# Taking the root of the query and key norms in two parts in a hybrid attention layer

## The chip, the cores and the metric

One Trainium2 chip, one core. The metric is the device time of one execution in microseconds; the times of the kernel before are 1372.91, 1371.18 and 1371.32 us, their median 1371.32 us. Engines are named as the profile names them: PE is TensorE (PEld its weight loads), DVE is VectorE, ACT is ScalarE, POOL is GpSimd, SP is SyncE, from whose queue nearly all DMAs are issued.

## The reference, cut to what matters

One decoder layer on 2048 tokens of width 1024: a pre-norm, one input projection, three attention branches side by side (latent attention with 8 heads, differential attention with 4 heads of two maps, cross-attention into 256 memory tokens), a gate, and one output projection. In the latent and in the differential branch every query and every key of every head is divided by the root of its mean square before (rotation and) the scores. These are the norms of this change:

```
def rms_norm(x, g, eps=RMS_EPS):
    xf = x.astype(jnp.float32)
    y = xf * lax.rsqrt(jnp.mean(xf * xf, axis=-1, keepdims=True) + eps)
    return (y * g.astype(jnp.float32)).astype(x.dtype)
# latent branch: heads of 64 plain and 32 rotated columns
    k = jnp.concatenate([k_nope, k_rope], axis=-1)
    q = rms_norm(q, qn_g)
    k = rms_norm(k, kn_g)
    q = jnp.concatenate([q[..., :MLA_NOPE], rope(q[..., MLA_NOPE:], pos)], axis=-1)
    k = jnp.concatenate([k[..., :MLA_NOPE], rope(k[..., MLA_NOPE:], pos)], axis=-1)
# differential branch: 8 maps of 32 columns
    q = rms_norm(dq.reshape(b, s, DIFF_HEADS * 2, DIFF_D), qn_g)
    k = rms_norm(dk.reshape(b, s, DIFF_HEADS * 2, DIFF_D), kn_g)
    q = rope(q, pos).reshape(b, s, DIFF_HEADS, 2, DIFF_D)
    k = rope(k, pos).reshape(b, s, DIFF_HEADS, 2, DIFF_D)
```

The inverse root doesn't depend on the rotation, so it can be multiplied on after it.

## The kernel before, in words

The work is cut into 28 steps: four blocks of 512 tokens for the memory branch (m), for two pairs of differential heads (d, 8 steps) and for four pairs of latent heads (a, 16 steps), in that order. Each step has a preparation (`prep_d`, `prep_a`) and then its attention maps. The maps run on PE (scores L572 or L917 to L919, values L516, L518, L536), ACT (the exponential p, L506) and DVE (its low half plo, L507). Beside them run the projections (L187 to L189), the gates, and late in the kernel the output projection (L958 to L960).

A preparation projects queries, keys and values, squares them (ACT), sums the squares (DVE) and takes the inverse root in `rstd_of` (L91 to L102) on POOL: one instruction adds the epsilon (L97) and one raises to the power -0.5 (L101). Then:

- `prep_d` (differential): the sums of 8 maps of queries and 8 of keys for 4 x 128 tokens lie in one tile of 32 columns, ss_d (L441). Keys are rotated first, then queries, on DVE (L354 to L358), each with a table that POOL makes (rt_d, L332 to L335); the table has one buffer, so that of the queries can be made only when the keys are rotated. One root for all 32 columns (r_d) stands between the two in the program. Then DVE multiplies the keys by it (L457), ACT and DVE split them into high and low halves (s_d, L465 and L466), SP transposes them by DMA (kT_d, L474), and the same follows for the queries (qB_d).
- `prep_a` (latent): the sums lie in ss_a, 8 columns of queries (L857) and 8 of keys (L854). POOL rotates the queries (L354 to L358), adds the part of the shared rotated key (L862), takes one root of 16 columns (r_a), and multiplies the rotated key by its 8 (L867, into kn_a). DVE multiplies the rest of the keys (L871) and then the queries (L873). Per head, ACT copies the high half of keys (ks_a, L878) and DVE takes the low half (L879), SP transposes (kT_a, L882), and so for queries (qs_a, L885 and L886, qB_a, L891).

After that the preparation estimates the largest score per query (`est_block`: PE L398, ACT L404 and L407, DVE L408 to L413), writes it into the queries, and transposes these again (L484, L900). Only then are the maps of the step free to start.

The order of the instructions on every engine is planned when the program is built, by priorities (a preparation goes ahead of what comes later in the list) and by planned times; on the chip every engine then works its own list strictly in that order, and waits where an operand isn't there. Preparations, maps and fills are woven into each other by due times (`Task`, L1110 onwards); a preparation is due 11 units (`LEAD`) ahead of its maps.

Of the kernel before, what the change touches and what calls it, by code (L numbers as in the profile page):

```python
# [11 lines left out]
F32 = mybir.dt.float32  # L12
# [4 lines left out]
ALU = mybir.AluOpType  # L17
AX = mybir.AxisListType

P = 128  # L20
# [12 lines left out]
def _bc(ap, axis, n):  # L33
    ap = ap.unsqueeze(axis)
    shape = list(ap.shape)
    shape[axis] = n
    return ap.broadcast_to(shape)
# [3 lines left out]
def hybrid_block(ctx: ExitStack, tc: tile.TileContext, x, mem, positions, norm_g, w_in, mla_q_norm_g,  # L41
# [3 lines left out]
    V, A, G, T, SP = nc.vector, nc.scalar, nc.gpsimd, nc.tensor, nc.sync  # L45
# [5 lines left out]
    sm = ctx.enter_context(tc.tile_pool(name="sm", bufs=2))  # L51
# [6 lines left out]
    def stack(shape, name):  # L58
        return wk.tile(shape, F16, tag="s2", name=name, bufs=6)
# [29 lines left out]
    gm = gain_cols(mem_norm_g, NK, "gm", WS, G)  # L89

    def rstd_of(ss, shape, name, tag="rstd", eps=EPS):  # L91
        r = sm.tile([P, 32 if tag == "rstd" else 8], F32, tag=tag, name=name)
        n = int(np.prod(shape))
        rv = r[:, 0:n]
        if len(shape) == 2:
            rv = rv.rearrange("p (a b) -> p a b", b=shape[1])
        G.tensor_scalar(rv, ss, eps, None, ALU.add)  # L97
        m = mhalf
        if len(shape) == 2:
            m = m.unsqueeze(2)  # L100
        G.tensor_tensor(rv, rv, m.broadcast_to([P] + list(shape)), ALU.pow)  # L101
        return rv  # L102
# [246 lines left out]
    def rope_in_place(q, tb, nh, eng, tmp):  # L349

        tmp = tmp.rearrange("p (t h d) -> p t h d", t=4, d=32)
        C = _bc(tb[:, 0], 2, nh)
        Sn = _bc(tb[:, 1], 2, nh)
        eng.tensor_tensor(tmp[..., 0:16], q[..., 16:32], Sn[..., 0:16], ALU.mult)  # L354
        eng.tensor_tensor(tmp[..., 16:32], q[..., 0:16], Sn[..., 16:32], ALU.mult)
        eng.tensor_tensor(q, q, C, ALU.mult)
        eng.tensor_tensor(q[..., 0:16], q[..., 0:16], tmp[..., 0:16], ALU.subtract)
        eng.tensor_tensor(q[..., 16:32], q[..., 16:32], tmp[..., 16:32], ALU.add)  # L358
# [18 lines left out]
    def new_qb(shape, name):  # L377
        return wk.tile(shape, F16, tag="qB", name=name, bufs=5)
# [45 lines left out]
    def prep_d(st, units):  # L424
        g, b, nm = st.g, st.b, st.name
# [14 lines left out]
        ss = sm.tile([P, 32], F32, tag="ss", name=f"ss_{nm}")  # L440
        V.reduce_sum(ss, sq.rearrange("p (a d) -> p a d", d=32), axis=AX.X)  # L441
        yield 1.0
        for w, gain in ((1, g_dk), (0, g_dq)):
            r4 = qk[:, :, 128 * w:128 * w + 128].rearrange("p t (m d) -> p t m d", d=32)
            rope_in_place(r4, rope_tabs(b, gain, f"{nm}{w}"), 4, V, sq[:, 512 * w:512 * w + 512])
            if w:
                r = rstd_of(ss, [32], f"r_{nm}").rearrange("p (t m) -> p t m", m=8)
            yield 2.0
        yield 1.0
        yield 1.0  # L450
# [3 lines left out]
        for w in (1, 0):  # L454
            r3 = qk[:, :, 128 * w:128 * w + 128]
            r4 = r3.rearrange("p t (m d) -> p t m d", d=32)
            V.tensor_tensor(r4, r4, _bc(r[:, :, 4 * w:4 * w + 4], 3, 32), ALU.mult)  # L457
            yield 1.0
            for i in range(2):
                dst = stack([P, 4, 2, 4, 32], f"s{w}{i}_{nm}")  # L460
                src = r4[:, :, 2 * i:2 * i + 2, :]
                G.memset(dst[:, :, :, 3, :], MS if w else 0.0)
                at_hi, at_lo = ((0, 2), 1) if w else ((0, 1), 2)
                for k in at_hi:
                    A.activation(dst[:, :, :, k, :], src, AF.Copy)  # L465
                V.tensor_tensor(dst[:, :, :, at_lo, :], src, dst[:, :, :, 0, :], ALU.subtract)  # L466
                if w:
                    out = kT[:, i].rearrange("p t m k -> p (t m) k")
                else:
                    qB = new_qb([P, 4, 2, P], f"qB{i}_{nm}")  # L470
                    st.qs.append(dst)
                    st.qB.append(qB)
                    out = qB.rearrange("p t m k -> p (t m) k")
                SP.dma_start_transpose(out, dst.rearrange("p t m r d -> p (t m r d)"))  # L474
                yield 1.0
# [348 lines left out]
    def prep_a(st):  # L824
        g, b, nm = st.g, st.b, st.name
# [24 lines left out]
        ss = sm.tile([P, 2, 8], F32, tag="ssa", name=f"ss_{nm}")  # L850
# [9 lines left out]
        rope_in_place(q[..., 64:96], tb, 2, G, sqt[:, 768:1024])  # L860
        s4 = ss[:, 1, :].rearrange("p (t h) -> p t h", h=2)
        G.tensor_tensor(s4, s4, _bc(ss_kr[b], 2, 2), ALU.add)  # L862
        r = rstd_of(ss.rearrange("p a b -> p (a b)"), [16], f"r_{nm}")
        rq = r[:, 0:8].rearrange("p (t h) -> p t h", h=2)
        rk = r[:, 8:16].rearrange("p (t h) -> p t h", h=2)
        yield 1.0
        G.tensor_tensor(kn[..., 64:96], _bc(krot[b], 2, 2), _bc(rk, 3, 32), ALU.mult)  # L867
        yield 1.0
        yield 1.0
        yield 1.0  # L870
# [227 lines left out]
    def a_prep(st):  # L1098
        if st.g == 0 and st.b == 0:
            yield from load_a_weights()  # L1100
        yield from prep_a(st)
# [102 lines left out]
    while True:  # L1204
# [26 lines left out]
        else:  # L1231
            mp, j, p0, h = heads.pop(0)
# [31 lines left out]
```

## Time and profile before

| | |
|---|---|
| median of the times | 1371.32 us |
| the profiled execution's own time | 1372.15 us |
| its span, first to last instruction | 1370.3 us |
| PE busy | 1293.0 us (94%) |
| DVE busy | 1123.1 us (82%) |
| ACT busy | 903.9 us (66%) |
| POOL busy | 333.9 us (24%) |
| mean granted TensorE clock | 0.989 |

Busy shares are means over stages with different limits. The memory steps and the loading of weights fill the first 150 us, the maps of the differential heads run until about 800 us with the preparations up to 640 us, and the preparations of the latent heads run from 640 to 1250 us. An engine's idle time costs something only where it makes PE, or the engine that PE waits for, stand.

### The profile page before, as it was taken

What the parts mean: (1) busy time and instruction counts of PE and PEld (TensorE: products, weight loads), DVE (VectorE), ACT (ScalarE), POOL (GpSimd) and SP (SyncE); (2) the same over time, 40 slices, a digit from 0 to 9 for tenths busy, and PEclk for the clock granted to TensorE, in tenths of its full rate; (3) what the DMA queues carried; (4) which work ended last, traced back from release to release, by engine and by line L of the source; (5) the groups of instructions that cost most, each with busy time, mean ns of one, the idle gap of its engine ahead of it and who ended that gap; (6) DMA issues with size and microseconds to landing.
All of it is one profiled execution on the core that took longest, in us unless ns stands there. A gap on an engine that the chain in (4) does not pass through costs nothing.

```text
span 1370.3 us, 35041 instructions
## 1 busy us (share of the span) xinstructions
PE 1293.0 (94%) x13616; PEld 829.5 (61%) x13616; DVE 1123.1 (82%) x2713; ACT 903.9 (66%) x2163; POOL 333.9 (24%) x477
## 2 busy tenths in 40 slices
PE   5988999999999999999998999999999998999998
PEld 2434556667667767667775656666655665655554
DVE  4657888879889867889899889999998998886745
ACT  6656544677878646786896667677766877665521
POOL 2322232403042133113202143223243323200000
PEclk9999999999999999999999999999999999999999
DMA  7998844223113322447446166347525643275452
GB/s 231 199 208 184 184 111 101 59 60 88 41 25 71 79 34 60 78 110 193 124 98 144 40 167 150 84 107 167 109 71 118 145 99 55 40 155 158 141 184 70
DMA packets 294262, 155.52 MB, mean 113 GB/s; under 512 B 239952, under 2 KB 272848, under 8 KB 294096
## 3 DMA queue, kind: packets, MB, share of 16 engines
q1 hardware_dynamic: 294064, 153.29, 47.7%
q8 instruction: 106, 1.74, 0.5%
q14 instruction: 60, 0.49, 0.1%
q0 software_dynamic: 32, 0.00, 0.0%
HBM read 61.75 MB, written 34.34 MB: 70 GB/s over the span
## 4 chain that ended last, share of the span: by engine, by line
PE 56%; DVE 13%; POOL 9%; ACT 8%; DMA 8%; issue 4%; SPq 1%; ACTq 0%; DVEq 0%; POOLq 0%
PE pp L189 6%; PE pp L187 6%; PE pp L188 6%; PE pe L398 5%; DVE plo L507 4%; PE pv L518 3%; PE pv L516 3%; PE pv L536 3%; PE st L572 3%; PE pp L958 3%; PE pp L959 3%; PE pp L960 3%; PE st L917 3%; PE st L918 2%; PE st L919 2%
## 5 line engine op out<-in xcount | busy, mean ns | idle before, releaser
L506 ACT ACTIVATE p<-st 128x512 f32<-128x512 f32 (+3 forms) x672 | 356.2, 551 | 167.2 <-PE st L919 65.8
L507 DVE TENSOR_TENSOR plo<-p 128x512 f16<-128x512 f32 (+3 forms) x672 | 404.6, 615 | 63.1 <-ACT p L506 59.2
L407 ACT ACTIVATE ec<-pe 128x512 bf16<-128x512 f32 (+3 forms) x384 | 197.2, 536 | 39.2 <-PE pe L400 17.1
L516 PEld LDWEIGHTS <-p 128*128 128x128 bf16 x2304 | 186.0, 99 | 51.5 <-DVE y_a L924 4.7
L518 PEld LDWEIGHTS <-p 128*128 128x128 bf16 x2304 | 173.1, 98 | 39.4 <-issue 4.1
L408 DVE TENSOR_TENSOR er<-er,ec 128x512 bf16<-128x512 bf16 (+3 forms) x384 | 141.5, 378 | 29.9 <-ACT ec L407 15.2
L404 ACT ACTIVATE er<-pe 128x512 bf16<-128x512 f32 x192 | 110.0, 606 | 47.2 <-DVE mx_a L413 18.1
L536 PEld LDWEIGHTS <-plo 128*128 128x128 f16 x2304 | 123.1, 97 | 23.7 <-DVE plo L507 5.8
L917 PE MATMUL st<-qB_a,kT_a 97*128 97x512 f16 (+1 forms) x320 | 112.8, 353 | 13.6 <-ACT p L506 8.7
L516 PE MATMUL pv<-V_d,p 128*128 128x65 f16 x1088 | 116.8, 194 | 3.3 <-DVE y_d L579 2.9
L189 PEld LDWEIGHTS <-ht_x 128*128 128x128 f16 x896 | 87.7, 98 | 52.9 <-ACT ht_x L137 3.9
L188 PEld LDWEIGHTS <-ht_x 128*128 128x128 f16 x896 | 87.8, 98 | 47.8 <-issue 4.0
L518 PE MATMUL pv<-V_d,p 128*128 128x64 f16 x1088 | 116.5, 196 | 0.0
L572 PE MATMUL st<-qB_d,kT_d 97*128 97x512 f16 (+1 forms) x320 | 111.4, 353 | 5.2 <-ACT zc L704 2.1
L187 PEld LDWEIGHTS <-ht_x 128*128 128x128 f16 x896 | 87.7, 98 | 47.1 <-issue 2.8
L516 PE MATMUL pv<-V_a,p 128*128 128x65 f16 x1088 | 112.6, 193 | 2.0 <-DVE y_a L924 1.9
L918 PE MATMUL st<-qB_a,kT_a 96*128 96x512 f16 (+1 forms) x320 | 112.6, 352 | 0.0
L398 PE MATMUL pe<-kT_d,qB_d 96*128 96x512 f16 (+2 forms) x320 | 106.2, 348 | 6.8 <-ACT ec L407 3.6
L518 PE MATMUL pv<-V_a,p 128*128 128x64 f16 x1088 | 112.2, 195 | 0.0
L919 PE MATMUL st<-qB_a,kT_a 96*128 96x512 f16 (+1 forms) x320 | 111.9, 350 | 0.0
L398 PE MATMUL pe<-kT_a,qB_a 96*128 96x512 f16 (+2 forms) x320 | 100.0, 349 | 7.7 <-DMA qB_a<-qs_a 4.6
L189 PE MATMUL pp<-w_d,ht_x 128*128 128x512 f16 x256 | 97.0, 379 | 0.0
(293 smaller groups left out, 3337.7 us busy)
## 6 DMA issues: line engine op xcount, KB each, us to landing
xt_x<-in_x_dram SPq DMA_DIRECT2D x16, 512.0 KB, 4.7
xr<-in_x_dram SPq DMA_DIRECT2D x16, 512.0 KB, 3.6
part<-xr SPq DMA_DIRECT2D x16, 512.0 KB, 2.9
ysc<-yt SPq DMA_DIRECT2D x31, 256.0 KB, 2.3
yl<-ysc SPq DMA_DIRECT2D x15, 512.0 KB, 4.6
zsc<-zc SPq DMA_DIRECT2D x48, 128.0 KB, 2.1
xa<-part SPq DMA_DIRECT2D x12, 512.0 KB, 3.6
out_dram<-xa SPq DMA_DIRECT2D x12, 512.0 KB, 2.9
```

Source lines behind the costliest of these rows:

```text
L187: T.matmul(ps[:, :n], lhsT=ht[:, 0, k], rhs=wt[:, 0, :n], start=(k == 0), stop=False)
L188: T.matmul(ps[:, :n], lhsT=ht[:, 0, k], rhs=wt[:, 1, :n], start=False, stop=False)
L189: T.matmul(ps[:, :n], lhsT=ht[:, 1, k], rhs=wt[:, 0, :n], start=False, stop=(k == NK - 1))
L398: T.matmul(ps[:, 0:n], lhsT=lhs(m, t), rhs=rhs(m, c, n // P), start=True, stop=c < b)
L407: A.activation(ec[:, 0:n], ps[:, 0:n], AF.Copy)
L506: A.activation(p32[:, :n], ps[:, :n], AF.Exp, scale=self.scale)
L507: V.tensor_tensor(plo[:, :n], p32[:, :n], phi[:, :n], ALU.subtract)
L516: T.matmul(pvv[:, t, 0:65], lhsT=phi[:, c], rhs=vt[:, 0:65], start=(j == 0 and t == 0), stop=False, skip_group_check=True)
L518: T.matmul(pvv[:, t, 0:64], lhsT=phi[:, c], rhs=vt[:, 65:129], start=False, stop=False, skip_group_check=True)
L536: last["pv"] = T.matmul(pvv[:, t, 0:65], lhsT=plo[:, c], rhs=vt[:, 0:65], start=False, stop=(j == self.njt - 1), skip_group_check=True)
L572: T.matmul(ps[:, :n], lhsT=st.kTs[j // 4][0:97, h, j % 4, m % 2, :], rhs=st.qB[h][0:97, t0:4, m % 2, :], start=True, stop=not diag)
L917: T.matmul(ps[:, :n], lhsT=kt[0:97, h, j % 4, 0, :], rhs=q[0:97, 0, t0:4, :], start=True, stop=False)
```

## The change

In both preparations the root is taken in two parts, each with its own L97 and L101: first the part of the keys, then the part of the queries. In `prep_d` each part follows the rotation of its half in the program, and its 16 columns lie 4 and 4 in a tile of 32 (a strided read). In `prep_a` the part of the keys needs only the sums of the keys; the part of the queries stands behind the product of the rotated key. The results get tiles of their own, in buffers of the same total size.

```
-        r = sm.tile([P, 32 if tag == "rstd" else 8], F32, tag=tag, name=name)
+        r = sm.tile([P, 16 if tag == "rstd" else 8], F32, tag=tag, name=name)
...
+        rs = {}
         for w, gain in ((1, g_dk), (0, g_dq)):
             r4 = qk[:, :, 128 * w:128 * w + 128].rearrange("p t (m d) -> p t m d", d=32)
             rope_in_place(r4, rope_tabs(b, gain, f"{nm}{w}"), 4, V, sq[:, 512 * w:512 * w + 512])
-            if w:
-                r = rstd_of(ss, [32], f"r_{nm}").rearrange("p (t m) -> p t m", m=8)
+            s4 = ss.rearrange("p (t w m) -> p t w m", w=2, m=4)[:, :, w, :]
+            r = rstd_of(s4, [4, 4], f"r{w}_{nm}", "rstd")
+            rs[w] = r
             yield 2.0
...
-            V.tensor_tensor(r4, r4, _bc(r[:, :, 4 * w:4 * w + 4], 3, 32), ALU.mult)
+            V.tensor_tensor(r4, r4, _bc(rs[w], 3, 32), ALU.mult)
...
-        r = rstd_of(ss.rearrange("p a b -> p (a b)"), [16], f"r_{nm}")
-        rq = r[:, 0:8].rearrange("p (t h) -> p t h", h=2)
-        rk = r[:, 8:16].rearrange("p (t h) -> p t h", h=2)
+        rk = rstd_of(ss[:, 1, :], [8], f"rk_{nm}", "rstd_k").rearrange("p (t h) -> p t h", h=2)
         yield 1.0
         G.tensor_tensor(kn[..., 64:96], _bc(krot[b], 2, 2), _bc(rk, 3, 32), ALU.mult)
+        rq = rstd_of(ss[:, 0, :], [8], f"rq_{nm}", "rstd_q").rearrange("p (t h) -> p t h", h=2)
         yield 1.0
```

## Rows read from the trace of the kernel before

**Rows 1.** Page, part 1: busy us (share of the span) and instructions of each engine.

```profile
PE 1293.0 (94%) x13616; PEld 829.5 (61%) x13616; DVE 1123.1 (82%) x2713; ACT 903.9 (66%) x2163; POOL 333.9 (24%) x477
```

**Rows 2.** Busy us (and instructions) by stage: columns PE, PEld, DVE, ACT, POOL, clock.

```profile
150.00:640.00 490.00, 480.47 (x5275) 328.15 (x5274) 415.21 (x1084) 330.15 (x860) 133.30 (x165) 1.00 0.36 79
640.00:1250.00 610.00, 575.09 (x6634) 380.09 (x6633) 544.94 (x1338) 437.68 (x1065) 162.59 (x223) 0.98 0.50 115
```

**Rows 3.** POOL's groups by shape: busy us, mean ns, then idle before.

```profile
L101 POOL TENSOR_TENSOR r_a<-r_a,mhalf 128x16 f32<-128x16 f32 x16 | 49.1, 3070 | 1.0
L101 POOL TENSOR_TENSOR r_d<-r_d,mhalf 128x32 f32<-128x32 f32 x8 | 44.4, 5544 | 0.7
L101 POOL TENSOR_TENSOR yr_d<-yr_d,mhalf 128x8 f32<-128x8 f32 x8 | 14.1, 1763 | 0.6
L97 POOL TENSOR_SCALAR r_a<-ss_a 128x16 f32<-128x16 f32 x16 | 6.1, 381 | 1.4
```

**Rows 4.** Waits around the roots: who for whom, us in total, times, longest.

```profile
ACT ks_a L878 <- POOL kn_a L867: 13.2, 10, 3.0
ACT s_d L465 <- DVE qkv_d L457: 11.3, 9, 4.6
DVE kn_a L871 <- POOL r_a L101: 7.0, 11, 1.2
```

**Rows 5.** PE's waits for the first queries (L398) and the exponential.

```profile
PE st L917 <- ACT p L506: 8.7, 13, 2.5
PE pe L398 <- DMA qB_a<-qs_a: 4.6, 3, 2.0
```

**Rows 6.** One latent preparation in order of time, on POOL.

```profile
787.09 2.94 POOL L101 TENSOR_TENSOR r_a<-r_a,mhalf 128x16 f32<-128x16 f32 x1
...
790.11 1.12 POOL L867 TENSOR_TENSOR kn_a<-krot,r_a 128x256 f32<-128x256 f32 x1
```

**Rows 7.** The same preparation on DVE.

```profile
790.06 0.69 DVE L871 TENSOR_TENSOR kn_a<-kn_a,r_a 128x512 f32<-128x512 f32 x1 [0.39 <-POOL r_a L101]
790.67 1.37 DVE L873 TENSOR_TENSOR qkv_a<-qkv_a,r_a 128x768 f32<-128x768 f32 x1
```

**Rows 8.** And on ACT, PE and SP (SPq is its queue).

```profile
791.26 0.52 ACT L878 ACTIVATE ks_a<-kn_a 128x384 f16<-128x384 f32 x1 [1.75 <-POOL kn_a L867]
793.74 0.38 PE L917 MATMUL st<-qB_a,kT_a 97*128 97x512 f16 x1 [0.57 <-ACT p L506]
793.85 1.81 SPq L882 DMA_TRANSPOSE kT_a<-ks_a  x1
795.84 1.50 SPq L891 DMA_TRANSPOSE qB_a<-qs_a  x1
799.39 0.39 PE L398 MATMUL pe<-kT_a,qB_a 96*128 96x512 f16 x1 [1.29 <-DMA qB_a<-qs_a]
```

**Rows 9.** All 16 products of queries: ns min/median/max, then busy us, mean ns.

```profile
L873 DVE TENSOR_TENSOR qkv_a<-qkv_a,r_a x16: 941/1369/1372, 682.6 to 1187.3; 128x768 f32<-128x768 f32 x16
...
L873 DVE TENSOR_TENSOR qkv_a<-qkv_a,r_a 128x768 f32<-128x768 f32 x16 | 19.2, 1201 | 0.0
```

**Rows 10.** One differential preparation: POOL, then DVE, then all 16 of L358 (mean ns).

```profile
391.95 5.68 POOL L101 TENSOR_TENSOR r_d<-r_d,mhalf 128x32 f32<-128x32 f32 x1
397.60 2.65 POOL L332 TENSOR_TENSOR rt_d<-cos_t,g_dq 128x64 f32<-128x64 f32 x1
...
396.11 0.41 DVE L358 TENSOR_TENSOR qkv_d<-qkv_d,sq_d 128x256 f32<-128x256 f32 x1
398.92 0.68 DVE L457 TENSOR_TENSOR qkv_d<-qkv_d,r_d 128x512 f32<-128x512 f32 x1
...
L358 DVE TENSOR_TENSOR qkv_d<-qkv_d,sq_d 128x256 f32<-128x256 f32 x16 | 7.0, 435 | 0.0
```

**Rows 11.** PE behind its longest late wait, and the ten us around it (columns of rows 2).

```profile
1040.71 0.58 PE L917 MATMUL st<-qB_a,kT_a 97*128 97x512 f16 x1 [2.54 <-ACT p L506]
...
1040.00:1050.00 10.00, 9.29 (x62) 4.63 (x62) 7.19 (x17) 4.66 (x11) 6.84 (x10) 0.66 0.30 67
```

## Prediction

> **What bounds the kernel now.** I read the page first, then the busy time by stage, then the groups of POOL, then the waits, then two preparations in order of time. The page gives PE 94% of the span and DVE 82% [rows 1]. By stage it is sharper: while the differential heads are prepared (150 to 640 us) PE is busy 480.5 of 490 us, so that only 9.5 us can be won there; while the latent heads are prepared (640 to 1250 us) PE is busy 575.1 of 610 and DVE 544.9 [rows 2]. There PE is free for 34.9 us and DVE for 65.1. So PE is the bound nearly everywhere, and the change can act only on the places where PE stands.
>
> POOL, at 24%, bounds nothing by its amount, but its roots stand in a chain. A root costs by its columns: 5.54 us for 32, 3.07 for 16, 1.76 for 8 [rows 3]. Behind it wait DVE, to multiply keys (7.0 us at L871), and ACT, to split them (13.2 us at L878 for POOL's product of the rotated key, 11.3 at L465 for DVE's product) [rows 4]. One latent preparation shows it whole: the root ends at 790.03, DVE starts on the keys at 790.06 and on the queries at 790.67, POOL's L867 ends at 791.23, ACT starts ks_a at 791.26 after standing 1.75 us [rows 6 to 8]. Then PE stands 0.57 us for an exponential that ACT had behind it in its list. Later PE stands 1.29 us for qB_a, the transposed queries; the keys' transpose was issued 2.0 us before theirs [rows 8]. So the queries, not the keys, end such a preparation.
>
> **The change, part by part.** I call the end of the root before T, here 790.03.
>
> Latent steps (16). The root of the keys has 8 columns, so it ends at T - 1.31 (3.07 - 1.76 [rows 3]). L867 starts 0.08 later and takes 1.12 [rows 6]: done at T - 0.11, against T + 1.20. L97 of the queries, 0.38, ends at T + 0.27, and their root at T + 2.03 [rows 3]. DVE now starts on the queries at T + 0.64 [rows 7]; that becomes T + 2.03, 1.39 later.
>
> There is a gain on DVE: the product of queries takes 0.94 us at best, 1.37 in the median, 19.2 us in all 16 [rows 9]. The median is what it takes beside L867 [rows 6, 7]; (19.2 - 16 x 0.94) / 0.43 is ten such steps. Behind the second root, L867 is long done: 0.94 each, 4.3 us less work on DVE. So the queries are multiplied by T + 2.97 against T + 2.01, 0.96 later.
>
> What each is worth on PE:
> - ACT's ten waits for L867 (13.2 us) get shorter by up to 1.31 each, about 13 us in all. In the one step shown 1.75 us of such a wait was followed by 0.57 us of PE, a share of 0.33; I take half of it, 0.16, since ACT has free time besides: 2.1 us won. Bounds: nothing, and all of PE's waits of this kind, 8.7 us [rows 5].
> - DVE's 4.3 us: if DVE's free time and PE's move together, 34.9 / 65.1 = 0.54 of it, 2.3 us; at the other end nothing. I take half, 1.2 us won.
> - The queries 0.96 us later: PE waits for them in front of the estimate 3 times, 4.6 us [rows 5], and each grows by as much: 2.9 us lost. It is less where DVE and ACT use the wait for the second root to split keys, which now stand between the queries' instructions. I take two of the three, 1.9 us lost; bounds nothing and 15.4 (all 16 steps). What covers the other 13 steps is the lead of the preparation; with that cover gone the upper bound holds.
>
> Differential steps (8). The keys' root of 16 columns takes 3.07 instead of 5.54, 2.47 us earlier. The sums are now read in runs of 4 from a tile of 32; no row shows that read, and its price lies between that of 16 columns side by side and that of 32 (5.54, then nothing is won). I take 3.07, the same number of elements. But the keys are rotated only by 396.52, 1.11 us before the root ended at 397.63 [rows 10], so in that step 1.1 us is all that can be won. Nine ACT waits at L465 times 1.1 is some 10 us of ACT; PE is free here for 9.5 us while ACT is free for 159.9 [rows 2], a share of 0.06: 0.6 us won. Bounds: nothing, and 3.3 us by the share of 0.33. The queries' root, if it goes straight behind the keys', ends at 391.95 + 3.07 + 0.38 + 3.07 = 398.5, and the queries' table would start then instead of at 397.60. Until they are multiplied they still need that table (2.65 us for its first instruction alone) and a rotation of five products, so their root is never what comes last. The table itself comes up to 0.9 us later, or 2.5 us earlier where it goes between the roots; I price both at nothing, because PE has the maps of the step before to run, and at 7.2 us (8 x 0.9) lost if that cover is gone.
>
> POOL does 16 x (2 x 1.76 + 0.38 - 3.07) + 8 x (2 x 3.07 + 0.38 - 5.54) = 13.3 + 7.8 = 21 us more, at 24% busy for nothing. No DMA is added or moved in the program, and SP's list keeps its number of issues. Each step gives DVE one more wait, in front of the queries' product: behind it queue the halves of keys (L879) and plo, for which PE's products of values wait.
>
> Sum: -2.1 - 1.2 + 1.9 - 0.6 = -2.0 us. The profiled execution took 1372.15 us (span 1370.3 and 1.85 around it), 0.83 above the median; so 1370.15 by it, and 1369.3 by the median.
>
> Beyond the sum: the lists of all engines are planned anew, and any later wait can grow or go. The scale of one such event is in the trace: PE stood 2.54 us at 1040.71, and in the ten us around it the granted clock was 0.66, that is 6.8 us at the lower of the two levels (1.2 and 2.4 GHz), or 3.4 us of lost work [rows 11]. One event is 3 to 6 us, more than the sum. That is why the range is wide.
>
> **A rule against the change.** While POOL's L867 ran, DVE's product took 0.43 us longer [rows 7, 9]. The Trainium skill (SBUF — State Buffer, "Who interferes with whom") says that a DVE instruction with two SBUF inputs and a GpSimd instruction that reads SBUF exclude each other, and that the later one is blocked for the whole of the other. By that rule every added root would hold DVE out. Against it, in the trace: L358, with two inputs in SBUF, took 0.41 us at 396.11, inside the 5.68 us root, and 0.435 in the mean of all 16 [rows 10]. The trace agrees for L867 and not for the roots.
>
> **Rivals.**
> - Faster by much (A root's wait is ACT's wait and ACT's wait is PE's). The full share holds, 0.33 of 13 us is 4.3, DVE gives 2.3, the differential steps 1.0, and the queries lose nothing because the keys' halves fill their wait: -7.6, so 1363.7. For it: PE's 0.57 us right behind ACT's 1.75 [rows 8]. Against it: ACT has 172 us free in that stage [rows 2], so most of its waits are free.
> - Slower: DVE stands for the second root. If the planner leaves the queries' product right behind that of the keys, as in ten steps now, DVE is done with keys at T - 1.31 + 0.03 + 0.69 = T - 0.59 and stands until T + 2.03: 2.6 us, 26 us in ten steps, in a stage where it is 89% busy. At 0.54 that is 14 us, at half of it 7; with 1.9 for the queries, less 2.7 won at ACT and in the differential steps, +6: about 1376.5 to 1377.5. It decides from the point where the plan takes the second root to be there within a us of the first. Against it: the plan is near the chip's times, since L871 waits 0.6 us in the mean [rows 4] behind a chain of many POOL instructions.
> - It doesn't do what it says: both roots are taken before L867, since both sums are there. L867 then ends at T + 2.03 instead of T + 1.20; ACT's ten waits grow by 0.83 each, 8.3 us, at 0.16 +1.3: about 1372.5.
> - POOL's added instructions hold DVE out: 21 us more of POOL, all of it DVE's, at 0.54 +11: 1382. Rows 10 speak against it.
>
> **How the numbers follow.** Forecast (a small gain, 1366.3 to 1372.3, at 1369.3): 0.42. Much faster: 0.23. DVE stands: 0.26. Both roots first: 0.06. DVE held out: 0.03. About 0.2%, 2.7 us, is what a measurement of this kernel can tell from no change. Of the forecast's 0.42 some 0.15 lies beyond that, 0.27 within. Faster 0.15 + 0.23 = 0.38; same 0.27 + 0.05 = 0.32; slower 0.26 + 0.01 + 0.03 = 0.30. The range of 1362 to 1379 leaves out the lower tail of the second case and the upper ends of the third and the last, together 0.18. Faster and same hold most of it, but slower is near, so the forecast's own range stands above.
>
> **What would show it.** POOL busy near 355 us. ACT's wait at L878 for L867 near zero; DVE's idle in front of L873, 0.0 now [rows 9], small if the plan fills it, tens of us in the third case. L873 near 0.94 us in nearly all steps. Roots of 8 columns at 1.76 us, of 16 at 3.07. L867 between the two roots. PE's wait for qB_a in front of L398 some 2 us longer. The prediction is wrong if PE's free time in 640 to 1250 us moves by over 6 us either way, and by its reasons if it moves far from the preparations.

## The result and the profile after

The kernel after takes 1413.3 us in the median (1407.6 to 1419.0), against 1372.1 (1371.2 to 1376.8) for the kernel before on the same chip: the ratio is 1.029, with a 95% interval of 1.0245 to 1.0341. It is 41 us slower, where a gain of 2.0 us was forecast.

The profiled execution took 1412.33 us, its span is 1410.6 us. Page, part 1: busy us, share of the span, instructions.

```profile
PE 1302.8 (92%) x13616; PEld 834.5 (59%) x13616; DVE 1123.5 (80%) x2713; ACT 901.8 (64%) x2163; POOL 365.6 (26%) x525
```

Against [rows 1] DVE and ACT have done the same work in the same time; POOL has 48 instructions and 31.7 us more. PE ran the same 13616 matmuls in 9.8 us more, and its idle time is 1410.6 - 1302.8 = 107.8 us against 1370.3 - 1293.0 = 77.3. So of the 40.3 us of span 30.5 are PE standing. The other 9.8 are PE busy for longer, and its lower mean granted clock, 0.982 against 0.989, accounts for about that: 1293.0 x 0.989 / 0.982 = 1302.2.

The same two stages as in [rows 2]: PE, PEld, DVE, ACT, POOL (busy us and instructions), clock.

```profile
150.00:640.00 490.00, 472.82 (x5121) 320.50 (x5118) 404.00 (x1056) 322.49 (x843) 139.34 (x173) 0.99 0.34 75
640.00:1250.00 610.00, 555.83 (x6395) 371.13 (x6395) 527.51 (x1301) 423.03 (x1044) 188.25 (x263) 0.98 0.47 107
```

The count of matmuls in a stage says about how far PE came. In the first it is 154 fewer of 5275, which at 490 / 5275 us each is 14 us; in the second 239 fewer of 6634, 22 us. Both stages lose.

POOL's groups by shape (busy us, mean ns, then idle before), to be read beside [rows 3]:

```profile
L101 POOL TENSOR_TENSOR r_d<-r_d,mhalf 128x16 f32<-128x16 f32 x16 | 57.1, 3580 | 0.6
L101 POOL TENSOR_TENSOR rk_a<-rk_a,mhalf 128x8 f32<-128x8 f32 x16 | 29.8, 1860 | 1.2
L101 POOL TENSOR_TENSOR rq_a<-rq_a,mhalf 128x8 f32<-128x8 f32 x16 | 27.9, 1746 | 0.1
L867 POOL TENSOR_TENSOR kn_a<-krot,rk_a 128x256 f32<-128x256 f32 x16 | 14.6, 913 | 0.9
L97 POOL TENSOR_SCALAR rk_a<-ss_a 128x8 f32<-128x8 f32 x16 | 13.8, 860 | 1.4
L97 POOL TENSOR_SCALAR rq_a<-ss_a 128x8 f32<-128x8 f32 x16 | 7.4, 464 | 1.3
```

The waits that answer to [rows 4] and [rows 5] (us in total, times, longest). L872 is the old L871, L874 the old L873, L879 the old L878, L918 the old L917; L354 and L538 belong to the rotation and to the products of values.

```profile
PE st L918 <- ACT p L508: 15.2, 17, 3.3
PE pv L538 <- DVE plo L509: 9.2, 10, 2.2
PE pe L398 <- DMA qB_a<-qs_a: 6.8, 3, 3.8
...
ACT ks_a L879 <- POOL kn_a L867: 23.6, 10, 3.8
DVE qkv_a L874 <- POOL rq_a L101: 14.0, 11, 2.0
DVE kn_a L872 <- POOL rk_a L101: 12.1, 11, 1.7
DVE sq_d L354 <- POOL rt_d L334: 8.8, 6, 3.6
```

ACT's wait for the rotated key, which was to go to nearly zero, has grown from 13.2 to 23.6 us. DVE now waits twice per step, 26.1 us in all against 7.0. And PE's waits for exponentials at the latent scores, 8.7 us before, are 15.2. (Not all of this belongs to the split: kernels with one root and newly planned lists, further down, show much of it too.)

**The latent steps: the queries' root goes first.** One latent preparation of the kernel after in order of time (start, duration): POOL, then DVE, then ACT.

```profile
834.29 0.56 POOL L97 TENSOR_SCALAR rq_a<-ss_a 128x8 f32<-128x8 f32 x1
834.93 0.32 POOL L335 TENSOR_TENSOR rt_a<-sin_t,g_q 128x64 f32<-128x64 f32 x1
835.21 0.20 POOL L864 TENSOR_TENSOR ss_a<-ss_a,sskr 128x8 f32<-128x8 f32 x1
835.37 1.78 POOL L101 TENSOR_TENSOR rq_a<-rq_a,mhalf 128x8 f32<-128x8 f32 x1
837.23 1.01 POOL L97 TENSOR_SCALAR rk_a<-ss_a 128x8 f32<-128x8 f32 x1
838.33 1.94 POOL L101 TENSOR_TENSOR rk_a<-rk_a,mhalf 128x8 f32<-128x8 f32 x1
840.35 1.12 POOL L867 TENSOR_TENSOR kn_a<-krot,rk_a 128x256 f32<-128x256 f32 x1
...
837.18 0.96 DVE L874 TENSOR_TENSOR qkv_a<-qkv_a,rq_a 128x768 f32<-128x768 f32 x1 [1.22 <-POOL rq_a L101]
840.30 0.69 DVE L872 TENSOR_TENSOR kn_a<-kn_a,rk_a 128x512 f32<-128x512 f32 x1 [0.76 <-POOL rk_a L101]
...
841.50 0.52 ACT L879 ACTIVATE ks_a<-kn_a 128x384 f16<-128x384 f32 x1 [3.69 <-POOL kn_a L867]
```

The program has the keys' part first; the plan of POOL's list has the queries' part first, in 13 of the 16 steps. In the other three the keys' root goes first, but in all 16 both roots are taken before L867, on which ACT waits. Here L867 starts 5.1 us after the in-place add of the keys' sums (L864) does. And a second thing is to be seen: the product of queries and the L97 of the keys start together, at 837.18 and 837.23, and that L97 takes 1.01 us. The same kernel's shortest takes 0.24, its median is 1.01:

```profile
L97 POOL TENSOR_SCALAR rk_a<-ss_a x16: 239/1010/1012, 703.0 to 1214.8; 128x8 f32<-128x8 f32 x16
L874 DVE TENSOR_TENSOR qkv_a<-qkv_a,rq_a x16: 945/959/1359, 702.9 to 1221.8; 128x768 f32<-128x768 f32 x16
```

(ns: shortest, median, longest.) POOL is held until DVE's product of 0.96 us is over.

Why the plan turned the order round could have been read in the kernel before. There, ACT's squares and then DVE's sums of one step:

```profile
672.78 0.90 ACT L855 ACTIVATE sqq_a<-qkv_a 128x768 f32<-128x768 f32 x1
673.52 0.47 ACT L853 ACTIVATE kn_a<-kn_a 128x256 f32<-128x256 f32 x1
...
673.72 0.95 DVE L857 TENSOR_REDUCE ss_a<-sqq_a 128x8 f32<-128x768 f32 x1
674.59 0.41 DVE L854 TENSOR_REDUCE ss_a<-kn_a 128x4 f32<-128x256 f32 x1
```

The queries' sums (L857) are there before the last of the keys' (L854), and the keys' sums need L862, the add, besides: in 11 of the 16 steps of that trace it is over more than 2 us after the queries' sums. With one root for both nothing hung on that. With two, the part whose operand is there first was given the place. The trace of the kernel after fits this step by step: in the 13 steps with the queries first their sums end over 2 us before the add is over, in the other three the add is over by then or within 0.1 us.

**The differential steps: the second root holds up the queries' table.** One differential preparation of the kernel after: POOL (x2 is both roots in one line), DVE, PE, and then all 16 roots.

```profile
385.69 10.21 POOL L101 TENSOR_TENSOR r_d<-r_d,mhalf 128x16 f32<-128x16 f32 x2
395.87 0.31 POOL L332 TENSOR_TENSOR rt_d<-cos_t,g_dq 128x64 f32<-128x64 f32 x1
...
391.93 0.68 DVE L459 TENSOR_TENSOR qkv_d<-qkv_d,r_d 128x512 f32<-128x512 f32 x1
392.74 0.41 DVE L509 TENSOR_TENSOR plo<-p 128x256 f16<-128x256 f32 x1
396.77 0.53 DVE L354 TENSOR_TENSOR sq_d<-qkv_d,rt_d 128x256 f32<-128x256 f32 x1 [3.62 <-POOL rt_d L334]
...
397.56 0.20 PE L538 MATMUL pv<-V_d,plo 128*128 128x65 f16 x1 [2.24 <-DVE plo L509]
...
L101 POOL TENSOR_TENSOR r_d<-r_d,mhalf x16: 2888/3138/7116, 182.6 to 634.0; 128x16 f32<-128x16 f32 x16
```

The two roots end at 395.90. DVE's unbroken row of products, all with two operands in SBUF, ends at 393.15, some 2.8 us earlier: about the 2.89 of the shortest root of this size. So the second root, 7.12 us by the profile, seems to have done its work only after that row was over. Then DVE stood 3.62 us for the table that had to be made behind the root, and PE 2.24 us for the low half plo, which stood behind the rotation in DVE's list.

### The profile page after: what moved, and what is told of

It is laid out like the page before. It is cut to its first block, busy times and chain, and to the rows that moved or that the text cites. A ratio compares the mean times of both kernels' runs of the same rounds, so it can differ in the third digit from the quotient of the medians.

```text
span 1410.6 us, 35091 instructions
## 1 busy us (share of the span) xinstructions
PE 1302.8 (92%) x13616; PEld 834.5 (59%) x13616; DVE 1123.5 (80%) x2713; ACT 901.8 (64%) x2163; POOL 365.6 (26%) x525
## 4 chain that ended last, share of the span: by engine, by line
PE 48%; DVE 17%; POOL 11%; DMA 10%; ACT 8%; issue 4%; SPq 1%; POOLq 0%; ACTq 0%; DVEq 0%
PE pp L187 5%; PE pp L189 5%; PE pp L188 5%; PE pe L398 5%; DVE plo L509 5%; POOL r_d L101 3%; PE pv L520 3%; PE pp L959 3%; PE pv L518 3%; PE pv L538 3%; PE pp L960 3%; PE pp L961 3%; PE st L574 2%; PE st L918 2%; DMA qB_a<-qs_a 2%
## 5 line engine op out<-in xcount | busy, mean ns | idle before, releaser
L408 DVE TENSOR_TENSOR er<-er,ec 128x512 bf16<-128x512 bf16 (+3 forms) x384 | 140.2, 375 | 31.7 <-ACT ec L407 16.3
L538 PEld LDWEIGHTS <-plo 128*128 128x128 f16 x2304 | 122.0, 98 | 30.9 <-DVE plo L509 14.4
L918 PE MATMUL st<-qB_a,kT_a 97*128 97x512 f16 (+1 forms) x320 | 113.1, 353 | 19.1 <-ACT p L508 15.2
L398 PE MATMUL pe<-kT_a,qB_a 96*128 96x512 f16 (+2 forms) x320 | 101.7, 352 | 11.9 <-DMA qB_a<-qs_a 6.8
L398 PE MATMUL pe<-kT_d,qB_d 96*128 96x512 f16 (+2 forms) x320 | 107.3, 350 | 5.2 <-ACT ec L407 3.1
```

What stands on the lines that cost most here:

```text
L398: T.matmul(ps[:, 0:n], lhsT=lhs(m, t), rhs=rhs(m, c, n // P), start=True, stop=c < b)
L408: V.tensor_tensor(er[:, t % 2, 0:n], er[:, t % 2, 0:n], ec[:, 0:n], ALU.max)
L538: last["pv"] = T.matmul(pvv[:, t, 0:65], lhsT=plo[:, c], rhs=vt[:, 0:65], start=False, stop=(j == self.njt - 1), skip_group_check=True)
L918: T.matmul(ps[:, :n], lhsT=kt[0:97, h, j % 4, 0, :], rhs=q[0:97, 0, t0:4, :], start=True, stop=False)
```

## The experiments

Sixteen kernels were run. In the table the ratio is to the kernel before on the same chip. The last two columns say how many us a kernel is behind at 640 and at 1250 us: the time at which PE had done the share of its work that it has done by then in the kernel before, each matmul counted with the median duration of its shape there. They come from one profiled execution each, so they are less certain than the ratio: e4_replan and e6_idle_d, which will turn out to have the same lists, stand at 17.2 and 28.0 at 1250 us, with medians 2 us apart.

| kernel | latent root | differential root | plan | ratio [95%] | behind at 640 | at 1250 |
|---|---|---|---|---|---|---|
| before | one | one | its own | 1 | 0 | 0 |
| e5_idle_a | one | one | as before | 0.9991 [0.9972, 1.0010] | -0.4 | -1.5 |
| e11_lead | one | one | new | 1.0104 [1.0077, 1.0131] | 1.9 | 13.8 |
| e13_idle_l | one | one | new | 1.0115 [1.0092, 1.0137] | 8.8 | 16.1 |
| e4_replan | one | one | new, that of e6_idle_d | 1.0155 [1.0118, 1.0192] | 4.8 | 17.2 |
| e6_idle_d | one | one | new, that of e4_replan | 1.0163 [1.0131, 1.0194] | 8.4 | 28.0 |
| e3_a_keys_first | keys first | one | new | 1.0053 [1.0032, 1.0074] | 0.4 | 7.2 |
| e9_idle_d_keys_first | keys first | one | new | 1.0104 [1.0075, 1.0133] | 5.3 | 19.4 |
| e14_lead_a_keys_first | keys first | one | new | 1.0119 [1.0092, 1.0147] | 2.8 | 10.0 |
| e2_a_only | queries first | one | new | 1.0150 [1.0116, 1.0184] | 0.1 | 28.0 |
| e15_lead_a | queries first | one | new | 1.0211 [1.0189, 1.0233] | 2.3 | 28.8 |
| e8_d_one_short | one | keys' alone | new | 1.0187 [1.0159, 1.0216] | 9.5 | 24.9 |
| e16_lead_d | one | split | new | 1.0200 [1.0170, 1.0230] | 10.7 | 26.2 |
| e7_d_tables_first | one | split, table first | new | 1.0224 [1.0189, 1.0258] | 9.4 | 32.0 |
| e1_d_only | one | split | new | 1.0258 [1.0232, 1.0283] | 17.3 | 36.5 |
| e10_both_keys_first | keys first | split | new | 1.0149 [1.0115, 1.0182] | 19.0 | 24.4 |
| e17_lead_both | queries first | split | new | 1.0241 [1.0216, 1.0266] | 11.3 | 27.7 |
| after | queries first | split | new | 1.0293 [1.0245, 1.0341] | 15.0 | 40.3 |

A point of the ratio, 0.01, is 13.7 us.

**One part alone.** e1_d_only has the differential split (with the smaller tile) and `prep_a` as before; e2_a_only has the latent split and `prep_d` as before.

> The change in the differential preparations alone; the latent ones keep one root. By the theory of the order (the loss is in the instruction order that the split gives on POOL, about 15 us of it by 640 us in the trace after, the rest behind it): about +15 us, 1385 to 1390. By the theory that all of it comes from the latent preparations, where the queries' root went ahead of the keys': within 3 us of before. By the theory that any new plan of this kernel's order costs much, whichever part is changed: +20 to +40.

> The change in the latent preparations alone; the differential ones keep one root. The plan puts the queries' root ahead of that of the keys here too. By the theory of the order: +20 to +28 us, 1392 to 1400, L867 about 2 us later behind the start of POOL's rotation than before, DVE waiting twice per preparation. By the rival that the differential half lost it all: within 3 us of before.

Measured: 1.0258, 35 us, and 1.0150, 21 us. Each part is slower by itself, and together they make 41, not 56: each alone already pays for newly planned lists, or they partly lose the same time. In e2_a_only the order is reversed as in the kernel after, DVE waits 15.5 us for the queries' root and ACT 25.0 for L867. In e1_d_only more than half of the loss, 19 us, arises between 640 and 1250 us, where `prep_a` is unchanged. No chain of the change explains that (the whole, +35, is in the third theory's range), and it asked for a measure of the plan itself.

**The keys' root held in front.** In e3_a_keys_first the latent split stands, and the queries' root is tied behind L867:

```
-        G.tensor_tensor(kn[..., 64:96], _bc(krot[b], 2, 2), _bc(rk, 3, 32), ALU.mult)
-        rq = rstd_of(ss[:, 0, :], [8], f"rq_{nm}", "rstd_q").rearrange("p (t h) -> p t h", h=2)
+        kr = G.tensor_tensor(kn[..., 64:96], _bc(krot[b], 2, 2), _bc(rk, 3, 32), ALU.mult)
+        with tc.issue_after(kr.ins):
+            rq = rstd_of(ss[:, 0, :], [8], f"rq_{nm}", "rstd_q").rearrange("p (t h) -> p t h", h=2)
```

> As the run with the latent part alone, but the queries' root is tied behind the product of the rotated key (L867), so that POOL works in the order that the change's words say. By the theory of the order the loss of the latent part goes: within 6 us of before either way, and ACT's wait for L867 falls below the 13.2 us of before. By the rival that two roots cost as such (DVE waits for two, or POOL's work holds DVE out), or that any new plan loses: still +15 us or more.

Measured: 1.0053, 6.4 us slower than before and 13 us faster than e2_a_only. In the program the two differ in the order alone; their lists are those of the kernel before up to some 680 us and differ from it, and from each other, on every engine behind that. PE's wait for exponentials at the latent scores is 5.7 us, against 14.8 in e2_a_only. The reversed order costs; but the order that the forecast assumed is no gain either. The other sign that was asked for did not come. ACT's wait for L867 (L865 here) did not fall below the 13.2 us of before:

```profile
ACT ks_a L878 <- POOL kn_a L865: 21.0, 11, 2.8
```

e10_both_keys_first is the kernel after with the same tie.

> The change with the one correction that the latent queries' root is tied behind L867. If the reversed order is a loss of its own, about 14 us as between the two latent runs (+20.8 and +6.4): +27 instead of +41. If it is the plan: anywhere from +20 to +45, and progress by 640 us as in the change itself (5121 matmuls from 150 to 640 us), since the plan is the same up to there.

Measured: 1.0149, half of the change's loss: +21 us, 20 less than the kernel after where 14 less was expected. The lists of the two are the same up to some 700 us (at 640 us the one execution was 19.0 behind, the other 15.0). Between 640 and 1250 us e10_both_keys_first loses 5.4 us, the kernel after 25.3. Its waits, and one of its preparations on POOL, the same as the one shown above:

```profile
ACT ks_a L880 <- POOL kn_a L867: 20.3, 9, 4.7
...
PE st L919 <- ACT p L508: 8.7, 12, 2.5
...
DVE qkv_a L875 <- POOL rq_a L101: 4.4, 8, 0.8
...
PE pe L398 <- DMA qB_a<-qs_a: 3.4, 3, 2.0
...
837.49 0.31 POOL L864 TENSOR_TENSOR ss_a<-ss_a,sskr 128x8 f32<-128x8 f32 x1
837.89 0.29 POOL L97 TENSOR_SCALAR rk_a<-ss_a 128x8 f32<-128x8 f32 x1
838.26 1.87 POOL L101 TENSOR_TENSOR rk_a<-rk_a,mhalf 128x8 f32<-128x8 f32 x1
840.21 1.12 POOL L867 TENSOR_TENSOR kn_a<-krot,rk_a 128x256 f32<-128x256 f32 x1
841.42 0.25 POOL L97 TENSOR_SCALAR rq_a<-ss_a 128x8 f32<-128x8 f32 x1
```

L867 starts 2.7 us after the add instead of 5.1; neither L97 is held up here (over all steps 3 of 32 take more than 0.6 us, 16 of 32 in the kernel after); DVE's wait for the queries' root falls from 14.0 to 4.4 us, and in the step shown DVE has a half of the keys and maximums to do in between; PE's wait for exponentials is back at 8.7 us, that for qB_a at 3.4. From the add to L867 the median of the 16 steps is 3.93 us in the kernel before, 5.15 after, 2.73 here. The forecast's gain of 1.31 taken off the 3.93 gives 2.62.

**A new plan with nothing else.** Four kernels ask what it costs that the lists are planned anew. They add one memset of 8 columns on POOL per preparation, which nothing reads (0.11 us each). As it depends on nothing, the plan does not leave it behind the root: the traces have all of them between 3.3 and 5.2 us, in nobody's way. e4_replan has them in both preparations, e5_idle_a in `prep_a` alone, e6_idle_d in `prep_d` alone, and e13_idle_l in the four query latents. e11_lead has no added instruction, only another due time:

```
+                G.memset(sm.tile([P, 8], F32, tag="idle", name=f"idle_{nm}"), 0.0)
...
-    LEAD = 11.0
+    LEAD = 11.5
```

> Before, with one more POOL instruction per differential and latent preparation behind the root, a memset of 8 columns that nobody reads (some 0.13 us each, 3 us in all on an engine with 24% busy). It shows what a new plan costs when nothing on any chain changes. By the theory of the order: within 5 us of before. By the theory that any new plan of this tuned order loses: +15 us or more.

> Before, with the memset that nobody reads in the latent preparations only. It is the neutral counterpart of the two runs that change the latent part alone (+20.8 and +6.4 us). If a new plan of the latent stage costs as such, whatever changed: +5 to +20, and then the keys-first order would be no loss but average. If the loss there is the split's own: within 4 us of before.

> Before, with the unread memset in the differential preparations only: neutral counterpart of the run with the differential half alone (+35). Theory that the split itself loses in the differential stage: PE does as many matmuls from 150 to 640 us as before (5275, give or take 60; 5092 with the split), and what is lost comes behind 640 us, by the new plan there, 0 to +20. Theory that a new plan loses everywhere: fewer matmuls by 640 us here too.

> Before, with the unread memset in the four query latents (some 500 to 630 us) only. The lists on DVE, ACT and SP stay as before up to about 500 us and are planned anew behind it. By the theory that a new plan of the latent stage costs as such: +10 to +25, all of it behind 640 us. By the theory that it takes a change of the roots: within 4 us, as where the memset stood in the latent preparations and the other engines' lists stayed as they were (-1.4).

> Before, with the lead of the preparations 11.5 instead of 11 units and nothing else: no instruction is added or taken away, and the lists of all engines are planned anew. If before's plan is one of the good ones among its neighbours and any other loses: +10 to +30. If the loss in the runs before is the root's own: within 5 us.

Measured: 1.0155, 0.9991, 1.0163, 1.0115 and 1.0104. The order of the instructions in the traces says which of them have a new plan:

- e5_idle_a has none. The lists of DVE, ACT, SP and, but for the memsets, POOL are those of before, and so is the time. It is no neutral counterpart of a new plan, as it was meant to be, but it shows that the same lists take the same time.
- e4_replan and e6_idle_d have one and the same plan: instruction for instruction on DVE, ACT, SP and, but for the memsets, POOL, and on PE but for 10 of 13616 places. Their ratios agree too.
- In e6_idle_d DVE's list leaves that of before at 241 us, in e11_lead at 170, in e13_idle_l at 535.

So these are three new plans in four kernels, and all three lose, 14 to 22 us; the mean of the three is 1.0126, 17 us. That the loss comes only behind 640 us, as one theory had it for e6_idle_d and for e13_idle_l, did not hold: by 640 us they are 1.9 to 8.8 us behind, and e6_idle_d has run 5193 matmuls from 150 to 640 us, not 5275 give or take 60. The plan of the kernel before is better than each of the three, and an edit that moves it starts with that loss, though not always with all of it: e3_a_keys_first has new lists from 680 us on and is 6.4 us behind, split included. Why one plan is better than another was not found. This is what the forecast had priced far too low.

The waits in these kernels also tell what of the kernel after is not the split's own. With one root as before, ACT's wait for L867 is 16.4 to 23.2 us in the four (23.6 after, 13.2 before), PE's for exponentials at the latent scores 7.5 to 15.2 (15.2 after, 8.7 before), and DVE's for the keys' root 13.7 to 15.4 (12.1 after, 7.0 before). e11_lead, for one:

```profile
ACT ks_a L878 <- POOL kn_a L867: 22.6, 11, 4.1
```

DVE's wait for the queries' root, 14.0 us after, is in none of them.

These kernels also show a root held out where nothing was split. POOL and DVE in e6_idle_d:

```profile
619.99 11.08 POOL L101 TENSOR_TENSOR r_d<-r_d,mhalf 128x32 f32<-128x32 f32 x1
...
625.09 0.68 DVE L508 TENSOR_TENSOR plo<-p 128x512 f16<-128x512 f32 x1
631.10 0.80 DVE L458 TENSOR_TENSOR qkv_d<-qkv_d,r_d 128x512 f32<-128x512 f32 x1 [5.34 <-POOL r_d L101]
```

A root of 32 columns, 5.44 us at its shortest in that kernel, took 11.08. It ended 5.3 us after DVE's last product (625.77), and DVE then had stood 5.34 us for it. e4_replan and e13_idle_l have such a root as well; the kernel before has none, its eight take 5.54 in the mean [rows 3], and neither has e11_lead, whose longest takes 5.73. So part of what a new plan costs can be of this kind, but e11_lead loses its 14 us without it.

**Keys first beside a neutral plan.** e9_idle_d_keys_first is e6_idle_d with the tie of e3_a_keys_first.

> The unread memset in the differential preparations, whose new plan alone cost +22, together with the latent split in the order of its words (queries' root tied behind L867), which alone cost +6.4. If what the split does by itself is small and the plan decides: between +5 and +30, with no rule that adds 22 and 6. If the keys-first split is a gain on any plan other than that of before: below +15. If the two add: +28.

Measured: 1.0104 against 1.0163, 8 us faster than the neutral kernel, +14 against before. The parts don't add; the two other theories both allow this. The lists of the two differ from some 690 us on, the intervals meet, and neutral plans differ by as much, so that a gain of the split with the keys in front is not shown.

**The differential root.** e7_d_tables_first is e1_d_only with the queries' root tied behind the queries' table (L335); e8_d_one_short is e1_d_only without a root of the queries, the queries being multiplied by that of the keys:

```
+            s4 = ss.rearrange("p (t w m) -> p t w m", w=2, m=4)[:, :, w, :]
             if w:
-                r = rstd_of(ss, [32], f"r_{nm}").rearrange("p (t m) -> p t m", m=8)
+                r = rstd_of(s4, [4, 4], f"r{w}_{nm}", "rstd")
+            rs[w] = r
```

> The differential half alone, with the queries' root tied behind the queries' table on POOL, so that the second root no longer stands in front of the table. By the theory that DVE loses its time at that table (8.8 us of waits for it after, 3.0 before, two of 3.5 us behind a second root that took 6 to 7 us): matmuls from 150 to 640 us back to 5275 or more, DVE's waits for the table below 3 us; the whole 0 to +20 by what the new plan does behind 640 us. If two roots cost as such or the new plan does: 5100 to 5200 matmuls again.

> The differential half alone with the keys' root of 16 columns taken and the queries' root left out: the queries are multiplied by the keys' root, so this part of the computation is changed. One POOL root fewer than the split, and half the columns of before. By the theory of the second root: 5275 or more matmuls from 150 to 640 us, and the most that an early keys' root can give in that stage, up to -3 us by 640. If the early product of keys itself disturbs DVE and ACT: still 5100 to 5200.

Measured: 1.0224 and 1.0187, against 1.0258 with the root in front of the table. In e7_d_tables_first the longest root is 3.46 us and DVE's wait for the table 3.5 us instead of 9.4; in e8_d_one_short there is no second root. Both are 8 us less behind at 640 us than e1_d_only (9.4 and 9.5 against 17.3). Of the whole time 5 and 10 us are won, the first within the intervals, the second beyond them. But neither gets back to the 5275 matmuls from 150 to 640 us that the theory of the second root asked for: they run 5168 and 5187, e1_d_only 5092, and the neutral plans 5184 to 5247. So what is left by 640 us is near what a new plan costs there, and so is the whole of e8_d_one_short, 1.0187, a little above the neutral plans. Their lists differ from those of e1_d_only from 187 us on, and the difference between plans is again as large.

**The same comparisons under another plan.** Each of these had rested on one plan. The lead of 11.5 gives another, with e11_lead as its neutral kernel; e14_lead_a_keys_first, e15_lead_a, e16_lead_d and e17_lead_both are e3_a_keys_first, e2_a_only, e1_d_only and the kernel after with that one line changed.

> The kernel before with a lead of 11.5 instead of 11, and the latent split with the keys' root held in front. The neutral kernel with that lead took 1386.95 us. Theory A (the order of the two roots is a matter of the chain and holds under any plan): L867 comes earlier, so this is not slower than the neutral one, 1375 to 1388, and ACT's wait for L867 is smaller than with the queries first under the same lead. Theory B (only the plan decides; the order's 14 us were scatter): anywhere between 1380 and 1400, with no relation to the next kernel.

> The same lead of 11.5 with the latent split as the change has it; the plan takes the queries' root first in most steps. Theory A: 8 to 20 us slower than the keys-first kernel of this lead, so 1390 to 1402. Theory B: within the scatter of plans, as likely faster as slower than the keys-first kernel.

> The same lead of 11.5 with the differential split alone. Theory C (the second root of 16 columns in front of the queries' table costs by itself, some 13 us beside what a new plan costs): 1396 to 1405, with a lag of 10 us or more against the kernel before by 640 us. Theory B (the plan alone): 1382 to 1395, and a lag by 640 us of 0 to 5 us as in the neutral kernels.

> The whole change with the lead of 11.5. Theory A and C together: 25 to 45 us above the neutral kernel of this lead if the parts add, 1412 to 1430; if they go beside each other as in the change itself, 1405 to 1415. Theory B: 1385 to 1405.

Measured: 1.0119, 1.0211, 1.0200, 1.0241. The order of the latent roots (theory A) holds (the plan has the queries' root first in 11 of the 16 steps of e15_lead_a): queries first is 0.0092 slower than keys first, 12.6 us, with intervals that don't touch, though these two again differ in all lists from some 685 us on, SP's from 733. Keys first equals the neutral kernel (1.0104). Between 640 and 1250 us the first loses 7.2 us and the second 26.5, as e3_a_keys_first (6.8) and e2_a_only (27.9) did under their plans. The stage and ACT's wait in the two, first e14_lead_a_keys_first:

```profile
640.00:1250.00 610.00, 569.55 (x6602) 378.03 (x6599) 538.91 (x1341) 437.07 (x1067) 178.63 (x255) 0.99 0.49 112
...
ACT ks_a L878 <- POOL kn_a L865: 20.1, 10, 6.1
```

and e15_lead_a:

```profile
640.00:1250.00 610.00, 561.24 (x6428) 370.70 (x6425) 528.01 (x1305) 427.60 (x1046) 184.41 (x255) 0.97 0.46 107
...
ACT ks_a L877 <- POOL kn_a L865: 34.7, 13, 6.0
```

174 matmuls fewer in the same stage, and 14.6 us more of ACT's wait. The differential split alone costs 0.0096 above the neutral kernel, 13 us, as it did in the first plan (1.0258 against 1.0163): theory C, with 10.7 us behind at 640 against 1.9. e17_lead_both is only 0.0137 above the neutral kernel, 19 us, less than its two parts (0.0107 and 0.0096) together. At 1404.0 us it lies below what theories A and C had and in the range of theory B; the parts don't add.

All kernels together bear the order out. By the last two columns of the table, from 640 to 1250 us the four with the keys first lose 5.4 to 14.1 us, the four with the queries first 16.4 to 27.9, and the eight with one latent root and new lists 7.3 to 22.6. So the order counts under every plan that was tried; whether the split with the keys first is better than one root under a new plan, these ranges, which overlap, don't show.

## Why the prediction was wrong

The sum was built step by step, and most of its durations hold. The time fails by two things that it took as given and one that it priced too low.

1. **The order of the two roots: the step that failed.** "The root of the keys has 8 columns, so it ends at T - 1.31" took the order from the program's text. The lists are ordered by planned times, and in the kernel before the queries' sums end first and the keys' still need an add, as the rows above show. Every figure of the latent part was computed for the order keys' root, L867, queries' root, and that occurred in none of the 16 steps. Where the order is forced, the figure is right (2.73 us from the add to L867 against 2.62), but not what was to follow from it: ACT's wait for L867, the sum's largest gain, is 17.1 to 21.0 us in the four kernels with the keys first, not near zero. The reversal costs 13 us under two plans (e2_a_only against e3_a_keys_first, e15_lead_a against e14_lead_a_keys_first) and 20 in the whole change (e10_both_keys_first). Among the rivals, "it doesn't do what it says" named what happened, both roots ahead of L867, in all 16 steps; it was given a chance of 0.06 and a price of +1.3 us, a tenth of the 13. Its share of 0.16 from ACT's wait to PE's can't be read off the kernel after: ACT's wait grew by 10.4 us, near the 8.3 it had, and PE's by 6.5, but the neutral plans show like growth of both with one root.

2. **"The lists of all engines are planned anew", sized at one event of 3 to 6 us.** [Rows 11] gave the size of one event; a new plan is many. Neutral edits cost 14 to 22 us. It was also taken as able to go either way; of three neutral plans none was faster than that of the kernel before. This term alone leads out of the range, and no row of one trace could have given it; what it needs is a neutral edit.

3. **The differential table, "priced at nothing", with 7.2 us if its cover is gone.** The cover was gone in part: in the traces DVE's wait for the table went from 3.0 to 8.8 us, PE's wait for plo from 2.1 to 9.2; in the neutral plans the two are 2.0 to 2.4 and 3.6 to 6.1. The root beside DVE's products was mis-sized as well: the mean of 16 columns is 3.58 us, not 3.07, because three of them took 4.5 to 7.1. The split costs 13 us above a neutral kernel in two comparisons (e1_d_only with e6_idle_d, e16_lead_d with e11_lead), of which e7_d_tables_first and e8_d_one_short put 5 to 10 on the second root. What makes up the rest stays open: the difference between plans is as large.

4. **The rule, weighed in one direction alone.** [Rows 10] show L358 at 0.41 us within a running root, so a running root doesn't hold DVE out, and that stands. But the same rows have the other direction: POOL's L332 took 2.65 us there, and 0.31 in the preparation shown above, where DVE stood. It was quoted as its duration. POOL is the side that can be held out, an L97 from 0.24 to 1.01 us, roots from 2.9 to 7.1 and from 5.4 to 11.1. The Trainium skill (SBUF — State Buffer, "Who interferes with whom") calls the ports that the two share an exclusive lock and says that issue order decides who blocks. The traces agree where DVE is first, but there the whole row of products passes, not one instruction; for a root that runs, [rows 10] don't show it.

5. **The rival "DVE stands for the second root"** named a wait that is there: 14.0 us in eleven steps, at the queries' product, against 26 in ten. But it was the first root, not the second, that DVE waited for at that product, and its +6 us is less than half of what the reversed order costs. When the keys go first, the plan fills much of that wait (4.4 us in e10_both_keys_first, 6.2 to 9.1 in the other three), as the forecast had hoped.

6. **What held.** Roots of 8 columns at 1.75 to 1.86 us (1.76 forecast); the strided read of 16 columns at no extra price (2.89 at the shortest); the product of queries at 0.96 us without L867 beside it, against 0.94; POOL at 366 us, against 355 (the roots of 16 columns and the L97 of `prep_a` took more than was reckoned, 8.0 and 9.0 us, L867 and others less).

How the 41 us divide was not separated. A new plan alone costs 14 to 22, the reversed order 13 to 20 more than the order keys first, and the differential split some 13 more than a neutral kernel. These add to more than 41, and plans differ among themselves by 8 us.

No version was found that beats the kernel before; the nearest with a split root is e3_a_keys_first, at +6.4 us.

## What to carry to other kernels

When a step is cut in two on an engine whose list is planned, the part whose operands are there first can be put first, whatever the program's order, as it was here: read in the trace of before when each operand ends, and tie the order if it matters. Before single microseconds are counted in such a kernel, run an edit that changes nothing but the plan, and see in the traces that the lists did change; here its cost was eight to nine times the forecast gain. And a duration in the trace is its work and its lock-out together: compare the shortest of the same form before it goes into a sum.

## What the hardware showed that was not expected

A steady row of DVE products with two operands in SBUF can keep a POOL instruction out until the row is over: a root that takes 2.9 us took 7.1 and ended 2.8 us after the row, and one of 5.4 us took 11.1 and ended 5.3 after it. It is the exception. In the 18 traces 143 roots of 8, 16 or 32 columns have DVE in such a row for all of their first 1.6 us, and 15 of them took over 1 us longer than the shortest of their size (2 of 11 in the kernel after); the root of [rows 10] is one of the others. Why one gets in and another doesn't stays open. A root under way did not slow DVE's products (0.41 us, [rows 10]). So moving a root by a few us can double its duration, although POOL is busy only 26% of the time.
